# Three small moves in a two-layer decoder trunk: GpSimd's weight sums tied to a norm's last scaling, one pair of transposes put earlier in the embedding, and the MLP's squares written by ScalarE

## The chip, the cores and the metric

The kernel runs on one core of one Trainium2 chip. The metric is the device time of the whole program in microseconds (us), on that core. A core has a matrix engine (TensorE, PE in the profile), three engines that work on vectors (VectorE, DVE; ScalarE, ACT; GpSimd, POOL), a synchronisation engine that issues transfers here (SP), and DMA queues. The engines run their own instruction lists in order and wait for one another through semaphores. Data lies in the on-chip SBUF (the program's "pages", 128 partitions by 512 words) and in the eight PSUM banks into which the matrix engine writes (the program's "banks").

## What is computed

A decoder trunk of two layers on 512 tokens of width 1024. Every sub-layer stands between two RMS norms. Cut to what matters:

```
for i in range(DEPTH):                       # DEPTH = 2
    g = norm_g[i]
    hn = rmsnorm(x, g[0])
    m = fox_attention(...) if i == 0 else short_conv(...)
    x = x + rmsnorm(m, g[1])
    f = jnp.square(jax.nn.relu(rmsnorm(x, g[2]) @ w_up)) @ w_down
    x = x + rmsnorm(f, g[3])
    gate = jax.nn.sigmoid(rmsnorm(x, g[4]) @ w_ple_gate[i])
    e = (p[i] @ w_ple_proj[i]) * gate
    x = x + rmsnorm(e, g[5])
```

The MLP is 1024 to 4096 and back; the last sub-layer is called the embedding below (`ple` in the kernel). Layer 0's mixer is an attention, layer 1's a short convolution.

## The kernel before, in words

**Products.** All matrix products are in full single precision, each as three passes over pairs of a high and a low part (`mm3`, lines 253 to 259): high by high on L255, two mixed ones on L256 and L257. The pair of parts is made by `split` (L261): ScalarE rounds a page to its high part (L263, `wh`, `hTh`, `A11h` ...), another engine subtracts that from the page (L264, `wl`, `hTl`, `A11l` ...). For most weights and for all activations the other engine is VectorE; for the weight sums of the MLP's second matrix, and for two of those of the convolution, it is GpSimd.

**Weights.** `fetch` issues transfers on SP into 14 buffers, `prepare` splits a weight some pages ahead of its use, and `derive` (L155 to L163) forms sums of weight blocks on GpSimd (`dn_T` for the MLP, `c_S` and `b_S` for the convolution), eight instructions for a group of the MLP. These sums exist since the MLP's second product and part of the convolution multiply 2 by 2 blocks by seven products instead of eight.

**A norm.** `pre_norm` (L310 on) runs for each of the four blocks of 128 tokens: ScalarE takes the sums of squares (L286, `junk`), GpSimd the reciprocal root (L278, L281), VectorE scales the block into two pages (`scaled`, L294, `n_h`; `n0b_h` in the norm ahead of the convolution), the matrix engine transposes them (L303, four transposes a page, into `n_p`), and `split` keeps them as `hTh` and `hTl`. The transposes are put off until 46,000 columns have streamed through the matrix engine (`put_off`, `due`), or until a product that reads them calls `need(t)` (L249).

**The MLP** (`mlp`, from L798). Eight groups of 512 hidden units. A group's up product gives four blocks f = 0 to 3: a relu from PSUM on ScalarE (L816, `r`), its square (L802, `q`, on VectorE), and from `q` the parts that the second product needs: `A11` and `A12` directly, `S1` to `S3` after sums on GpSimd (`s`, L830). `down` has 84 matrix instructions a group in groups 0 to 6, seven products in the order of `STEPS`. In group 0 the up product runs in two halves of 256 tokens (16 squares of 128x256 in the two layers) and ScalarE copies the results out to `acc` (L859); in groups 1 to 6 VectorE adds them (L862). Group 7 is plain: ScalarE writes the high part of the square as a square (`hh`, L892), VectorE writes the square again (`q`, L893 by L802) and subtracts (`hl`, L895); meanwhile GpSimd brings the seven sums together (`combine`, L869).

**The embedding** (`ple`, from L919). Four early blocks of `pp`, six matrix instructions each, need nothing of the norm. Then come the eight blocks of `pg`, 24 instructions each, in the order of `BLOCKS`; each begins with `need(t)`. Token block 0 is the first.

**What sets the order.** A scheduler that simulates the program orders each engine's instructions, but keeps what a data dependence or a dependence added by hand asks for. So a change of an engine or of a wait can move rows elsewhere too.

Of the kernel before, what the change touches and what calls it, by code (L numbers as in the profile page):

```python
# [10 lines left out]
AF = mybir.ActivationFunctionType  # L11
ALU = mybir.AluOpType
# [22 lines left out]
FEW = 4  # L35
BLOCKS = ((0, 0), (1, 0), (0, 1), (1, 1), (2, 1), (3, 1), (2, 0), (3, 0))
EARLY = 4
BY_HAND = 2
LEFT = 10
LATE = 0  # L40
# [27 lines left out]
def trunk(ctx: ExitStack, tc, x, pT, g, wv, wqk, bf, wo, wci, wcq, cw, wco, wup, wdn, wpp, wpg, out):  # L68
    nc = tc.nc
# [9 lines left out]
    def page(name, dtype=F32):  # L79
        return pages.tile([P, S], dtype, tag="pg", name=name)  # L80

    def bank(name):
        return psum.tile([P, S], F32, tag="ps", name=name)
# [10 lines left out]

    loads, order, where, ready, fetched, begun = [], [], {}, {}, [], [0]
    derived, recipes = {}, {}

    def plan(key, src):
        where[key] = len(order)
        order.append((key, len(loads)))  # L100
        loads.append(src)
# [45 lines left out]
    def fetch(upto):  # L147
        while len(fetched) < min(upto, len(loads)):
            n = len(fetched)
            raw = raws.tile([P, S], F32, tag="raw", name=f"raw{n}")  # L150
            fetched.append(raw)
            src = loads[n]
            nc.sync.dma_start(raw[:, : src.shape[-1]], src)

    def derive(key):  # L155
        at, sums = recipes.pop(key)
        fetch(max(at.values()) + 1)
        B = {name: fetched[n][:, :S] for name, n in at.items()}
        for name, a, b, op in sums:
            t = page("_".join(str(u) for u in (*key, *name)))  # L160
            derived[(*key, *name)] = t
            B[name] = t[:, :S]
            nc.gpsimd.tensor_tensor(out=B[name], in0=B[a], in1=B[b], op=op)  # L163

    def prepare(upto):
        while begun[0] < min(upto, len(order)):
            n = begun[0]
            begun[0] += 1
            key, at = order[n]
            for of in (key[:3], key[:2]):  # L170
                if of in recipes:
                    derive(of)
            hi, lo = page(f"wh{n}", F32R), page(f"wl{n}", F32R)
            if isinstance(at, tuple):
                raw, w = derived.pop(key), S
                eng = nc.gpsimd if key[0] == "dn" or key[-1] in ON_POOL else nc.vector
            else:
                fetch(at + 1)
                raw, eng, w = fetched[at], nc.vector, loads[at].shape[-1]
                fetched[at] = None  # L180
            split(hi[:, :w], lo[:, :w], raw[:, :w], eng)
            ready[key] = Pair(hi[:, :w], lo[:, :w])

    def wide(*key, soon=SOON):

        prepare(where[key] + 1 + soon)
        return ready[key]
# [61 lines left out]
    def need(*keys):  # L249
        while any(k in keys for _, k, _ in later):  # L250
            later.pop(0)[2]()

    def mm3(ps, a, b, start, stop):

        nc.tensor.matmul(ps, a.hi, b.hi, start=start, stop=False)  # L255
        nc.tensor.matmul(ps, a.lo, b.hi, start=False, stop=False)  # L256
        nc.tensor.matmul(ps, a.hi, b.lo, start=False, stop=stop)  # L257
        streamed[0] += 3 * ps.shape[-1]
        due()
# [24 lines left out]
    def squares(src, name):  # L284
        ss = stat(name)
        nc.scalar.activation(junk, src, AF.Square, scale=D**-0.5, accum_out=ss)  # L286
        return ss
# [3 lines left out]

    def scaled(t, n, xs, r, gB, name):
        h = page(f"{name}_h{t}_{n}")
        nc.vector.scalar_tensor_tensor(  # L294
            out=h[:, :S], in0=xs[n][:, :S], scalar=r, in1=gB[n][:, :S],
            op0=ALU.mult, op1=ALU.mult,
        )
        return h

    def turned(t, n, h, name):  # L300
# [9 lines left out]
    def pre_norm(t, xs, gB, hT, name, also=lambda t, n, ps: None):  # L310

        r = stats(t, xs, name)
        hs = [scaled(t, n, xs, r, gB, name) for n in range(2)]

        def turn():
            for n in range(2):
                ps = turned(t, n, hs[n], name)
                keep(t, n, ps, hT)
                also(t, n, ps)

        put_off(t, turn)
# [7 lines left out]
    def gained(m, gB, n, name, out=None):  # L329

        mg = page(name) if out is None else out
        nc.vector.tensor_tensor(out=mg[:, :S], in0=m, in1=gB[n][:, :S], op=ALU.mult)
        return mg

    def residual(t, mg, sums, xs, name):

        r = rstd(sums, f"{name}_r{t}")
        for n in range(2):
            nc.vector.scalar_tensor_tensor(  # L339
                out=xs[n][:, :S], in0=mg[n][:, :S], scalar=r, in1=xs[n][:, :S],  # L340
                op0=ALU.mult, op1=ALU.add,
            )
# [8 lines left out]
    def tokens_of(pair, t):  # L351
        return pair.at(lambda h: h[:, t * P : (t + 1) * P])

    def tokens(pair, k, t):
        return pair.at(lambda h: h[:, k, t * P : (t + 1) * P])

    def soon(t, n):

        return FEW if n else SOON
# [19 lines left out]
    def attention(hT, first_x, g0, by_hand):  # L379
# [224 lines left out]
        def rows(t):  # L604
            r = stats(t, first_x[t], name)
            return [scaled(t, n, first_x[t], r, g0, name) for n in range(2)]
# [48 lines left out]
        for c in range(-8, n_sc + LAG):  # L655
            if c == n_sc - BY_HAND:
                by_hand.enter_context(tc.manual_schedule(engines={E.PE}))
# [140 lines left out]
    def mlp(l, hT, xs, then, late):  # L798
        acc = {}

        def square(out, r):
            nc.vector.tensor_tensor(out=out, in0=r, in1=r, op=ALU.mult)  # L802

        def up(gr, done, soon=lambda f: SOON):
            for lo, hi in ((0, 256), (256, 512)) if gr == 0 else ((0, 512),):
# [69 lines left out]
        for gr in range(7):  # L875
            A, s, q = {}, {}, {f: page(f"q{l}_{gr}_{f}") for f in range(4)}

            def done(f, lo, hi, r):
                square(q[f][:, lo:hi], r[:, : hi - lo])
                if lo == 0 and f % 2 == 0:  # L880
                    halves(gr, f, ("A11",), q[f], A)
                if hi == S:
                    quarters(gr, f, q, s, A)

            up(gr, done)
            down(gr, A)
# [3 lines left out]
        def done(f, lo, hi, r):  # L890
            h = Pair(*(page(f"h{s}{l}_{f}", F32R) for s in "hl"))
            nc.scalar.activation(h.hi[:, :S], r[:, :S], AF.Square)  # L892
            sq = page(f"q{l}_{f}")  # L893
            square(sq[:, :S], r[:, :S])
            nc.vector.tensor_tensor(  # L895
                out=h.lo[:, :S], in0=sq[:, :S], in1=h.hi[:, :S].bitcast(F32), op=ALU.subtract
            )
            hs.append(h)
            if f == LATE:
                gB.extend(late())  # L900

        up(7, done, lambda f: SOON + 2 * f)
        for t in range(NB):
# [6 lines left out]
            for n in range(2):  # L910
                a = total[t, n][:, :S]
# [7 lines left out]
    def ple(l, hT, xs, gB, then):  # L919
        def proj(t, n):  # L920
            pe = bank(f"pp{l}_{n}_{t}")
            for k in range(2):
                mm3(
                    pe, tokens_of(wide("p", l, k), t),
                    wide("pp", l, n, k), k == 0, k == 1,
                )
            return pe

        early = [proj(t, n) for t, n in BLOCKS[:EARLY]]
        mgs, sums = {}, {}  # L930
        for t, n in BLOCKS:
            need(t)
            if (t, n) == (2, 0):
                prepare(where["pg", l, 1, KT - 1] + 1 + SOON)
            pe = early.pop(0) if early else None
            if pe is None and l == 1 and (t, n) == BLOCKS[-1]:
                pe = proj(t, n)
            ps = bank(f"pg{l}_{n}_{t}")
            for k in range(KT):
                w = wide("pg", l, n, k, soon=soon(t, n))  # L940
                mm3(ps, tokens(hT, k, t), w, k == 0, k == KT - 1)
            gate = page(f"gate{l}_{n}_{t}")
            nc.scalar.activation(gate[:, :S], ps, AF.Sigmoid)
            pe = pe or proj(t, n)
            e = page(f"e{l}_{n}_{t}")
            nc.vector.tensor_tensor(out=e[:, :S], in0=pe, in1=gate[:, :S], op=ALU.mult)
            sums[t, n] = squares(e[:, :S], f"es{l}_{n}_{t}")
            mgs[t, n] = gained(e[:, :S], gB, n, f"em{l}_{n}_{t}")
            if (t, 1 - n) in mgs:
                residual(t, *([d.pop((t, i)) for i in range(2)] for d in (mgs, sums)), xs[t],  # L950
                         f"er{l}")
                then(t)
# [24 lines left out]
    for l in range(2):  # L977
# [46 lines left out]
        else:  # L1024

            def then(t):
                for n in range(2):
                    nc.sync.dma_start(
                        out[t * P : (t + 1) * P, n * S : (n + 1) * S], xs[t][n][:, :S]
                    )  # L1030

        ple(l, h4, xs, g5, then)


# [59 lines left out]
```

## Time and profile before

| | us |
|---|---|
| median of 3 runs | 1248.64 (1248.42 to 1248.65) |
| the profiled execution | 1249.44 |
| its span in the trace | 1247.4 |
| mean granted TensorE clock | 0.996 of full |

The profile is of one execution. A row of the timeline reads: start in us from the span's start, duration in us, engine, line, operation, output and inputs, shapes, and how many; in square brackets the idle time ahead of it and what ended that. Matrix instructions are pipelined: a 128x512 one has a duration of about 0.39 us, yet the next one starts 0.227 us later where nothing is waited for, and that spacing is what counts. A row of the waits reads: who waited, for whom, total us, times, longest. A row of the groups reads: line, engine, operation, names, shapes, count, busy us, mean ns, idle us ahead and what ended it. A row of the chain of waits reads: start, us, engine, line.

### The profile page before, as it was taken

To read this page: it belongs to the slowest core of one execution; us is meant where nothing else is said; L and a number is where in the kernel's file an instruction comes from. 1 tells how busy PE (TensorE), PEld (TensorE's weight loads), DVE (VectorE), ACT (ScalarE), POOL (GpSimd) and SP (SyncE) were. 2 spreads that over 40 slices of the span, in tenths; PEclk is the share of its full clock that TensorE was granted. 3 is DMA by queue.
4 is the path that set the end of the run, shared out by engine and by line. 5 is a ranking of instruction groups with operands and counts; after the bars stand their busy time and mean duration, and the time that the engine had idled before them with its cause. 6 is when DMAs were issued, how large, how long until landed. Compare 5 with 4: busy or idle time off the path is not lost.

```text
span 1247.4 us, 18644 instructions
## 1 busy us (share of the span) xinstructions
PE 1218.7 (98%) x6188; PEld 1030.8 (83%) x6188; DVE 973.7 (78%) x1466; ACT 632.4 (51%) x1357; POOL 692.7 (56%) x667
## 2 busy tenths in 40 slices
PE   7999999999999999999999999999999999999997
PEld 6888887887888888887788999989778888888786
DVE  5657878676789778989878798867788788779972
ACT  5456777546544543454565544544655344535451
POOL 2017667257878776775213255227777878778210
PEclk9999999999999999999999999999999999999999
DMA  7465554532343224428223033542422343236401
GB/s 253 148 159 167 152 156 115 183 121 80 98 135 111 83 77 135 136 68 271 84 85 105 32 102 98 161 164 68 135 68 78 126 136 107 65 100 192 146 18 51
DMA packets 85792, 148.72 MB, mean 119 GB/s; under 512 B 10112, under 2 KB 17328, under 8 KB 85696
## 3 DMA queue, kind: packets, MB, share of 16 engines
q1 hardware_dynamic: 85488, 147.27, 37.5%
q8 instruction: 49, 0.80, 0.3%
q14 instruction: 47, 0.39, 0.1%
q10 hardware_dynamic: 144, 0.26, 0.1%
q0 software_dynamic: 64, 0.00, 0.0%
HBM read 136.93 MB, written 6.37 MB: 115 GB/s over the span
## 4 chain that ended last, share of the span: by engine, by line
PE 71%; DVE 11%; ACT 5%; issue 5%; POOL 4%; DMA 3%; SPq 1%; DVEq 0%; POOLq 0%; ACTq 0%
PE up L255 7%; PE up L257 7%; PE up L256 7%; PE dn L256 6%; PE dn L257 6%; PE dn L255 6%; DVE wl L264 4%; ACT junk L286 2%; PE qk L255 2%; PE qk L256 2%; PE qk L257 2%; PE pg L255 2%; PE pg L256 2%; PE pg L257 2%; DVE n_h L294 1%
## 5 line engine op out<-in xcount | busy, mean ns | idle before, releaser
L264 DVE TENSOR_TENSOR wl<-raw,wh 128x512 fp32r<-128x512 f32 (+1 forms) x398 | 379.2, 1000 | 26.9 <-ACT wh L263 25.8
L263 ACT CAST wh<-raw 128x512 fp32r<-128x512 f32 (+1 forms) x398 | 217.1, 619 | 10.9 <-DVE xd L339 5.0
L256 PE MATMUL up<-hTh,wl 128*128 128x512 f32 (+1 forms) x576 | 210.1, 365 | 0.0
L257 PE MATMUL up<-hTl,wh 128*128 128x512 f32 (+1 forms) x576 | 209.8, 366 | 0.0
L255 PE MATMUL up<-hTh,wh 128*128 128x512 f32 (+1 forms) x576 | 209.3, 366 | 0.0
L264 POOL TENSOR_TENSOR wl<-dn_T,wh 128x512 fp32r<-128x512 f32 x112 | 160.9, 1470 | 35.8 <-ACT wh L263 29.5
L256 PEld LDWEIGHTS up<-hTh,wl 128*128 128x128 f32 x576 | 108.6, 189 | 17.5
L257 PEld LDWEIGHTS up<-hTl,wh 128*128 128x128 f32 x576 | 108.3, 189 | 17.8 <-DVE hTl L264 0.2
L255 PEld LDWEIGHTS up<-hTh,wh 128*128 128x128 f32 x576 | 108.6, 189 | 17.4
L862 DVE TENSOR_TENSOR acc<-dn,acc 128x512 f32<-128x512 f32 x168 | 107.4, 679 | 7.7 <-PE dn L257 7.7
L163 POOL TENSOR_TENSOR dn_T<-raw,raw 128x512 f32<-128x512 f32 x56 | 87.9, 1581 | 39.3 <-DMA raw<-in_wdn 26.4
L816 ACT ACTIVATE r<-up 128x512 f32<-128x512 f32 (+1 forms) x72 | 38.7, 547 | 119.6 <-PE up L257 119.6
L163 POOL TENSOR_TENSOR dn_T<-raw,dn_T 128x512 f32<-128x512 f32 x56 | 91.8, 1638 | 2.2
L802 DVE TENSOR_TENSOR q<-r 128x512 f32<-128x512 f32 (+1 forms) x72 | 70.4, 985 | 27.1 <-ACT r L816 26.7
L263 ACT CAST A11h<-q 128x256 fp32r<-128x256 f32 x28 | 11.4, 407 | 103.2 <-DVE q L802 103.2
L263 ACT CAST wh<-dn_T 128x512 fp32r<-128x512 f32 x112 | 61.2, 617 | 0.0
L255 PE MATMUL pg<-wh,hTh 128*128 128x512 f32 x128 | 51.5, 402 | 3.6 <-ACT hTh L263 3.6
L869 POOL TENSOR_TENSOR acc<-acc,acc 128x512 f32<-128x512 f32 x28 | 47.1, 1716 | 8.7 <-DVE acc L862 8.7
L255 PE MATMUL qk<-hTh,wh 128*128 128x512 f32 x128 | 51.1, 399 | 0.0
L256 PE MATMUL pg<-wh,hTl 128*128 128x512 f32 x128 | 50.9, 398 | 0.0
L257 PE MATMUL qk<-hTl,wh 128*128 128x512 f32 x128 | 50.8, 397 | 0.0
L257 PE MATMUL pg<-wl,hTh 128*128 128x512 f32 x128 | 50.8, 397 | 0.0
(372 smaller groups left out, 3237.0 us busy)
## 6 DMA issues: line engine op xcount, KB each, us to landing
raw<-in_wup SPq DMA_DIRECT2D x128, 256.0 KB, 2.8
raw<-in_wdn SPq DMA_DIRECT2D x128, 256.0 KB, 2.8
raw<-in_wcq SPq DMA_DIRECT2D x36, 256.0 KB, 3.0
raw<-in_wqk SPq DMA_DIRECT2D x32, 256.0 KB, 3.4
raw<-in_wpg SPq DMA_DIRECT2D x32, 256.0 KB, 3.5
g<-in_g SPq DMA_DIRECT2D x22, 256.0 KB, 5.6
prl<-neg_c SPq DMA_DIRECT2D x16, 256.0 KB, 6.5
raw<-in_wo SPq DMA_DIRECT2D x16, 256.0 KB, 4.3
```

Source lines behind the costliest of these rows:

```text
L163: nc.gpsimd.tensor_tensor(out=B[name], in0=B[a], in1=B[b], op=op)
L255: nc.tensor.matmul(ps, a.hi, b.hi, start=start, stop=False)
L256: nc.tensor.matmul(ps, a.lo, b.hi, start=False, stop=False)
L257: nc.tensor.matmul(ps, a.hi, b.lo, start=False, stop=stop)
L263: nc.scalar.copy(hi, src)
L264: eng.tensor_tensor(out=lo, in0=src, in1=hi.bitcast(F32), op=ALU.subtract)
L286: nc.scalar.activation(junk, src, AF.Square, scale=D**-0.5, accum_out=ss)
L294: nc.vector.scalar_tensor_tensor(out=h[:, :S], in0=xs[n][:, :S], scalar=r, in1=gB[n][:, :S], op0=ALU.mult, op1=ALU.mult,)
L802: nc.vector.tensor_tensor(out=out, in0=r, in1=r, op=ALU.mult)
L816: nc.scalar.activation(r[:, :n], ps[:, :n], AF.Relu)
L862: nc.vector.tensor_tensor(out=a, in0=banks[s], in1=a, op=ALU.add)
L869: nc.gpsimd.tensor_tensor(out=a, in0=a, in1=acc[i, s][:, :S], op=ALU.add)
```

## The change

Three edits. First, `scaled` remembers its VectorE instruction in `last_norm`, and the first GpSimd sum that `derive` issues after it gets a dependence on that instruction. In the program's order this concerns the sums of MLP group 0 in both layers (after the second `n_h` of the last token block) and one of the convolution's `c_S` sums (after the last `n0b_h`). GpSimd's list itself keeps its order.

Second, in the embedding `need(BLOCKS[0][0])`, which issues the transposes of token block 0, stands ahead of the third early `pp` block.

Third, `square` is an activation on ScalarE: 72 instructions leave VectorE's list, 56 of 128x512 and 16 of 128x256, and join ScalarE's.

```
+TURNED = 2
...
+    last_norm = []
...
-            nc.gpsimd.tensor_tensor(out=B[name], in0=B[a], in1=B[b], op=op)
+            ins = nc.gpsimd.tensor_tensor(out=B[name], in0=B[a], in1=B[b], op=op)
+            if last_norm:
+                tc.add_manual_dep(
+                    ins.ins, last_norm.pop().ins.name,
+                    mybir.DependencyInfo(mybir.DependencyClass.Sync, mybir.DependencyReason.DATA),
+                )
...
     def scaled(t, n, xs, r, gB, name):
         h = page(f"{name}_h{t}_{n}")
-        nc.vector.scalar_tensor_tensor(
+        last_norm[:] = [nc.vector.scalar_tensor_tensor(
             out=h[:, :S], in0=xs[n][:, :S], scalar=r, in1=gB[n][:, :S],
             op0=ALU.mult, op1=ALU.mult,
-        )
+        )]
         return h
...
         def square(out, r):
-            nc.vector.tensor_tensor(out=out, in0=r, in1=r, op=ALU.mult)
+            nc.scalar.activation(out, r, AF.Square)
...
-        early = [proj(t, n) for t, n in BLOCKS[:EARLY]]
+        early = []
+        for i, (t, n) in enumerate(BLOCKS[:EARLY]):
+            if i == TURNED:
+                need(BLOCKS[0][0])
+            early.append(proj(t, n))
```

The matrix engine's list at the start of layer 0's embedding, before: the end of the third early block `pp_1_0`, the transposes of token block 0 (two rows of four), the fourth early block, and the first product that needs the transposed tokens.

```order
L257 MATMUL pp_1_0_7232<-wl_6935,wh_6865 128x512
L303 MATMUL n_p_0_7239<-ident,n_h_0_7050 128x128 x4
L303 MATMUL n_p_1_7246<-ident,n_h_1_7052 128x128 x4
L255 MATMUL pp_1_1_7253<-wh_6922,wh_6853 128x512
L256 MATMUL pp_1_1_7253<-wh_6922,wl_6854 128x512
L257 MATMUL pp_1_1_7253<-wl_6923,wh_6853 128x512
L255 MATMUL pp_1_1_7253<-wh_6934,wh_6865 128x512
L256 MATMUL pp_1_1_7253<-wh_6934,wl_6866 128x512
L257 MATMUL pp_1_1_7253<-wl_6935,wh_6865 128x512
L255 MATMUL pg_0_0_7260<-wh_6956,hTh 128x512
```

The same place now (nine lines lower in the file): the end of the second early block, the transposes, and the third early block, after which the six rows of the fourth and `pg` follow.

```order
L266 MATMUL pp_0_1_7225<-wl_6890,wh_6865 128x512
L312 MATMUL n_p_0_7232<-ident,n_h_0_7050 128x128 x4
L312 MATMUL n_p_1_7239<-ident,n_h_1_7052 128x128 x4
L264 MATMUL pp_1_0_7246<-wh_6922,wh_6853 128x512
L265 MATMUL pp_1_0_7246<-wh_6922,wl_6854 128x512
L266 MATMUL pp_1_0_7246<-wl_6923,wh_6853 128x512
L264 MATMUL pp_1_0_7246<-wh_6934,wh_6865 128x512
L265 MATMUL pp_1_0_7246<-wh_6934,wl_6866 128x512
L266 MATMUL pp_1_0_7246<-wl_6935,wh_6865 128x512
```

The transposes moved up by six matrix instructions: 12 stand between them and the first `pg` instead of six.

ScalarE's list at the same place, before: sums of squares of the MLP's result (`fs`) and of the new residual (`n_q`, from `xd`), and the casts of the two transposed pages.

```order
L286 ACTIVATE junk,fs_2_0_7134<-acc_4_0_4128 128x512
L286 ACTIVATE junk,fs_2_1_7136<-acc_5_0_4158 128x512
L286 ACTIVATE junk,n_q_2_7146<-xd_2_0_6779 128x512
L263 CAST hTh<-n_p_0_7239 128x4x128
L286 ACTIVATE junk,n_q_2_7148<-xd_2_1_6781 128x512
L263 CAST hTh<-n_p_1_7246 128x4x128
```

And now:

```order
L295 ACTIVATE junk,fs_2_0_7134<-acc_4_0_4128 128x512
L295 ACTIVATE junk,fs_2_1_7136<-acc_5_0_4158 128x512
L272 CAST hTh<-n_p_0_7232 128x4x128
L272 CAST hTh<-n_p_1_7239 128x4x128
L295 ACTIVATE junk,n_q_2_7146<-xd_2_0_6779 128x512
L272 CAST hTh<-n_p_0_7315 128x4x128
```

Both casts moved ahead of the sums of squares of token block 2's residual.

ScalarE's list in MLP group 2 of layer 0, before: relu `r`, and the casts from the square `q`, which VectorE writes.

```order
L263 CAST A11h0_2_0_4740<-q0_2_0_4660 128x256
L816 ACTIVATE r0_2_1_0_4771<-up0_2_1_0_4746 128x512
L263 CAST A12h0_2_1_4774<-q0_2_1_4661 128x512
L263 CAST S1h0_2_1_4782<-s120_2_1_4778 128x512
L263 CAST S3h0_2_1_4786<-s340_2_0_4744 128x512
```

And now:

```order
L811 ACTIVATE q0_2_0_4660<-r0_2_0_0_4737 128x512
L272 CAST A11h0_2_0_4740<-q0_2_0_4660 128x256
L825 ACTIVATE r0_2_1_0_4771<-up0_2_1_0_4746 128x512
L811 ACTIVATE q0_2_1_4661<-r0_2_1_0_4771 128x512
L272 CAST A12h0_2_1_4774<-q0_2_1_4661 128x512
```

The square stands between the relu that it reads and the cast that reads it, on the same engine.

## The prediction

> **What bounds the kernel now.** The page first: which engine is busy nearly always?
>
> ```profile
> span 1247.4 us, 18644 instructions
> PE 1218.7 (98%) x6188; PEld 1030.8 (83%) x6188; DVE 973.7 (78%) x1466; ACT 632.4 (51%) x1357; POOL 692.7 (56%) x667
> ```
>
> The matrix engine is the bound, and no edit takes one of its instructions away. So the change can win only where that engine stands still, runs late or runs slow. The second view is therefore the list of its waits, cut to the places that the edits reach:
>
> ```profile
> PE pg L255 <- ACT hTh L263: 3.6, 2, 1.9
> PE n_p L303 <- DVE n_h L294: 2.3, 4, 1.1
> PE dn L256 <- DVE hl L895: 2.1, 2, 1.2
> PE c L256 <- DVE wl L264: 1.5, 1, 1.5
> PE dn L256 <- DVE A12l L264: 0.6, 2, 0.3
> ```
>
> Together 10.1 us. The other waits of the list lie in the start and in the attention, which no edit touches. A wait list misses small delays and a slow clock, so the third view is the timeline at each of these places, read by the starts of consecutive instructions. For that one needs the spacing where nothing is waited for. A stretch of MLP groups 0 and 1 gives it (columns: window, length, then busy time and count of each engine, granted clock, DMA share):
>
> ```profile
> 306.00:350.00 44.00, 43.73 (x192) 35.56 (x191) 36.29 (x40) 28.88 (x56) 31.95 (x25) 1.00 0.34 104
> ```
>
> 192 matrix instructions in 44.00 us, less one short wait of 0.3, are 0.227 us each.
>
> **Edit 2, the embedding's start.** The matrix engine around the first `pg` of each layer:
>
> ```profile
> 607.64 0.40 PE L257 MATMUL pp<-wl,wh 128*128 128x512 f32 x1
> 609.74 0.50 PE L255 MATMUL pg<-wh,hTh 128*128 128x512 f32 x1 [1.71 <-ACT hTh L263]
> ...
> 1183.43 0.40 PE L257 MATMUL pp<-wl,wh 128*128 128x512 f32 x1
> 1185.76 0.50 PE L255 MATMUL pg<-wh,hTh 128*128 128x512 f32 x1 [1.93 <-ACT hTh L263]
> ```
>
> From start to start 2.10 and 2.33 us instead of 0.227: 1.87 and 2.10 lost, 4.0 together. Why is `hTh` late? ScalarE and VectorE in layer 0:
>
> ```profile
> 608.50 0.63 ACT L286 ACTIVATE junk<-xd 128x512 f32<-128x512 f32 x1 [2.95 <-DVE xd L339]
> ...
> 609.12 0.57 ACT L263 CAST hTh<-n_p 128x512 fp32r<-128x512 f32 x1
> ```
>
> ```profile
> 607.66 1.40 DVE L339 SCALAR_TENSOR_TENSOR xd<-acc,mr_r_y,xd 128x512 f32<-128x512 f32 x2
> ```
>
> ScalarE stood idle for 2.95 us, not for the transposes but for `xd`, the residual of another token block, whose sum of squares is queued ahead of the cast. The order shows that both casts now stand ahead of that sum, and that 12 products instead of six lie between the transposes and `pg`. Six more products are 6 x 0.227 = 1.4 us of cover, and the 2.95 us of ScalarE's idling lie ahead of the casts: together they exceed the 1.71 and 1.93 us waited. Both waits go: **4.0 us**. What is moved late is only that sum of squares; it feeds the norm of block 2, whose transposes come several blocks of `pg` (24 x 0.227 = 5.4 us each) later. Bounds: nothing, if the transposes themselves come to wait for `n_h`, and 4.0.
>
> **The clock behind it.** In layer 1 the wait is followed by slow products. Two adjoining windows:
>
> ```profile
> 1183.56:1186.98 3.42, 1.49 (x9) 1.08 (x8) 2.08 (x4) 2.47 (x7) 0.47 (x2) 1.00 0.01 2
> 1186.98:1190.39 3.41, 3.41 (x10) 2.64 (x9) 3.41 (x6) 1.54 (x5) 1.87 (x3) 0.50 0.00 0
> ```
>
> In the second the granted clock is 0.50 for 3.41 us, so half of it, 1.7 us, is lost. In the window ahead of it the matrix engine was busy for 1.49 of 3.42 us. I read this as the price of the wait in layer 1: without it that window is full, and the clock stays. **1.7 us**; bounds 0 and 1.7. The Trainium skill (TensorE: Matmul & The Clock Gate, "HAM oscillation") has the rule that the clock falls only after idle gaps of over about 3.4 us. This trace does not agree: the gap was 1.93 us. By that rule the slow stretch would have another cause and stay, and the sum would be smaller by its 1.7 us; that is the third rival.
>
> **Edit 1, GpSimd's sums wait.** The chain of waits holds the scalings ahead of both MLPs; the one of 256.29 is the same two instructions for an earlier token block:
>
> ```profile
> 256.29 1.42 DVE n_h L294 x2
> ...
> 270.67 3.46 DVE n_h L294 x2
> ...
> 671.87 1.77 DVE n0b_h L294
> ...
> 847.14 3.46 DVE n_h L294 x2
> ```
>
> ```profile
> 270.60 2.97 POOL L163 TENSOR_TENSOR dn_T<-raw,raw 128x512 f32<-128x512 f32 x2
> ```
>
> The slow pairs (3.46 against 1.42) ran beside GpSimd's first sums, which began 0.07 us earlier. With the wait the scaling takes 1.42, 2.0 us less, and the matrix engine's 2.3 us for `n_p` go. But the sums start at about 272.1 instead of 270.60. Eight of them end later by that 1.5 us less what their own undisturbed speed gives back, and behind them on GpSimd are the low parts of the first weights of `down`. So part of the gain may be handed on to group 0's `down`. That already loses time:
>
> ```profile
> 289.12 0.40 PE L255 MATMUL dn<-wh,A11h 128*128 128x512 f32 x1
> ...
> 310.49 0.39 PE L255 MATMUL up<-hTh,wh 128*128 128x512 f32 x1
> ...
> 865.61 0.40 PE L255 MATMUL dn<-wh,A11h 128*128 128x512 f32 x1
> ...
> 886.98 0.39 PE L255 MATMUL up<-hTh,wh 128*128 128x512 f32 x1
> ```
>
> 84 instructions take 21.37 us in either layer; 84 x 0.227 are 19.07, so 2.3 are lost in each, 4.6 in both. Its waits are for parts made from late squares, which leads to the third edit.
>
> **Edit 3, squares on ScalarE.** In group 0:
>
> ```profile
> 284.35 2.17 ACT L263 CAST wh<-dn_T 128x512 fp32r<-128x512 f32 x4
> ...
> 288.21 0.93 ACT L816 ACTIVATE r<-up 128x256 f32<-128x256 f32 x3
> 291.44 0.62 ACT L263 CAST A12h<-q 128x512 fp32r<-128x512 f32 x1 [2.30 <-DVE q L802]
> ```
>
> ```profile
> 289.23 2.18 DVE L802 TENSOR_TENSOR q<-r 128x256 f32<-128x256 f32 x3
> ```
>
> ScalarE finished three relus at 289.14 and idled 2.30 us for squares that VectorE made one after another beside GpSimd. Done on ScalarE at a relu's price (0.93 / 3 = 0.31) the three relus and squares end at 288.21 + 6 x 0.31 = 290.1, so `A12h` comes 1.4 us earlier. For norm and group 0 together 2.3 + 4.6 = 6.9 us are at stake. I take the norm's 2.3 in full and about half of the 4.6, since the later sums hold back the casts of their results (284.35), which ScalarE has queued ahead of group 0's last relus: **4.5 us**; bounds 0 and 6.9.
>
> In groups 1 to 6 a square costs ScalarE what the existing one (`hh`) costs, and it leaves VectorE, where it cost more:
>
> ```profile
> L802 DVE TENSOR_TENSOR q<-r 128x512 f32<-128x512 f32 x56 | 58.6, 1047 | 23.3 <-ACT r L816 23.0 <-issue 0.2
> ...
> L892 ACT ACTIVATE hh<-r 128x512 fp32r<-128x512 f32 x8 | 5.1, 632 | 0.4
> ```
>
> ```profile
> ACT A11h L263 <- DVE q L802: 103.2, 28, 7.0
> ...
> ACT A12h L263 <- DVE q L802: 41.8, 28, 2.3
> ```
>
> The chain relu, square, cast becomes 0.4 us shorter, and ScalarE's 145.0 us of idling for squares hold the 56 x 0.632 = 35.4 us of new work. In these groups the matrix engine waited only for `A12l`, 0.6 us in group 1 of both layers, with a VectorE list that now lacks a square of 1.05 us: **0.6 us**; bounds 0 and 0.6.
>
> In group 7:
>
> ```profile
> 582.22 0.39 PE L257 MATMUL dn<-wl,hh 128*128 128x512 f32 x1
> 583.86 0.50 PE L256 MATMUL dn<-wh,hl 128*128 128x512 f32 x1 [1.25 <-DVE hl L895]
> ...
> 1158.76 0.39 PE L257 MATMUL dn<-wl,hh 128*128 128x512 f32 x1
> 1159.96 0.50 PE L256 MATMUL dn<-wh,hl 128*128 128x512 f32 x1 [0.81 <-DVE hl L895]
> ```
>
> 1.64 and 1.20 instead of 0.227: 1.41 and 0.97, together **2.4 us**. Ahead of that `hl` VectorE loses three squares at 1.05, over 3 us of queue, while ScalarE adds one of 0.63 to each block: I take it in full. Bounds 0 and 2.4.
>
> The convolution waits 1.5 us for a weight's low part on VectorE, which was queued behind the slowed `n0b_h` (1.77; half of 1.42, 0.71, elsewhere) at the start of its own sums. With the sums held back two scalings are 2.1 us shorter; later sums still run beside later subtractions. I take **1.3 us**; bounds 0 and 1.5.
>
> **The sum.** 4.0 + 1.7 + 4.5 + 0.6 + 2.4 + 1.3 = 14.5 us. The profiled execution took 1249.44 (2.0 around the span of 1247.4), so 1234.9; the median of the runs is 0.8 below it: **1234.1 us**. What a measurement of this kernel can tell from no change is about 0.2%, 2.5 us.
>
> **The rivals.**
>
> *Stalls move.* The matrix engine comes earlier to group 0 and to the convolution, where the weights' low parts come no earlier, since GpSimd started later. Then 4.5 and 1.3 are given back: 8.7 us stay, 1239.9. For it: the sums begin 1.5 us later. Against: they then run without VectorE beside them. Chance 0.17.
>
> *The wait is passed on with its full length.* As before, and each of the two groups 0 starts its `down` 1.5 us later still: 8.7 - 3.0 = 5.7 us, 1242.9. Against: ScalarE casts the first results of the sums only at 284.35, so the sums' late start must first use up that slack. Chance 0.06.
>
> *The slow clock stays*, because a wait elsewhere or the window's place causes it: 14.5 - 1.7 = 12.8, 1235.8. For it: 1.71 us of waiting in layer 0 had no such stretch behind it, so the wait alone does not make one. Chance 0.08.
>
> *All is given back*: ScalarE's longer list delays relus, weight casts or `hTh` at many places by a little. About 1248. Chance 0.04.
>
> *Slower: ScalarE's list becomes the path in groups 1 to 6.* It takes its list in order, so a square behind a relu delays the next weight cast by 0.63. Were the matrix engine to wait for those, four squares in each of 12 groups would cost 12 x 4 x 0.632 = 30 us: about 1264. It decides from 14.5 / 12 = 1.2 us lost in each group. Against it: ScalarE was busy for 28.88 of 44.00 us in the window above, and a group of 180 products (40.9 us) adds 2.5 to its 27. Chance 0.04.
>
> **How the numbers follow.** The forecast has 0.61. The range reaches below to all of the 6.9 and 1.5 us, 2.6 more than taken, and a little of work no longer slowed elsewhere: 1230.5. Above it reaches just over the first rival: 1240.5. This holds the forecast's case, the slow clock's and most of the first rival's: about 0.8. Faster by over 0.2%: 0.61 + 0.17 + 0.08 + 0.06 = 0.92; within: 0.04; slower: 0.04.
>
> **What the changed profile would show.** Right: no wait of `pg` for `hTh`, no half clock at 1187; both `n_h` pairs at 1.4 us; no wait for `hl`; `down` of group 0 under 20.5 us; ScalarE near 54% and VectorE near 73% busy. The group 0 step is wrong if `down` stays over 21 us or if the matrix engine waits for `wl` made from `dn_T`. The whole is wrong if it waits in groups 2 to 6, where it has not waited: for `r`, `A11h` or a `wh`.

## The result, and the profile after

The changed kernel takes 1237.30 us, the median of 5 runs (1236.94 to 1237.49); the kernel before, 1248.64 in the runs beside them (5 runs, 1246.40 to 1251.19). The ratio is 0.9908, with a 95% interval from 0.9897 to 0.9918: 11.3 us faster, inside the range of the prediction, and 3.2 us above its number. The page after:

```profile
span 1235.8 us, 18684 instructions
PE 1213.4 (98%) x6188; PEld 1030.6 (83%) x6188; DVE 896.5 (73%) x1394; ACT 676.1 (55%) x1429; POOL 686.8 (56%) x667
```

VectorE lost 77 us of work and ScalarE gained 44, about as costed, and the span lost 11.6. The matrix engine's waits now (the rows left out lie in the start and in the attention):

```profile
...
PE dn L264 <- ACT r L825: 1.1, 2, 0.9
...
PE n_p L312 <- DVE n_h L303: 0.8, 1, 0.8
PE dn L265 <- DVE S1l L273: 0.8, 2, 0.4
PE c L264 <- DVE za L761: 0.7, 1, 0.7
...
PE dn L265 <- DVE A12l L273: 0.4, 1, 0.4
PE up L266 <- DVE hTl L273: 0.3, 1, 0.3
```

The rows of `pg` for `hTh` and of `dn` for `hl` are gone. The one `n_p` wait left is that of the kernel's start. The waits for the relu `r`, in group 0 of both layers, have risen from 0.5 to 1.1 us, and those for `S1l` and `za` are new. The two starts of the embedding after, `pg` right behind the last `pp` in both layers:

```profile
604.74 0.39 PE L266 MATMUL pp<-wl,wh 128*128 128x512 f32 x1
604.96 0.40 PE L264 MATMUL pg<-wh,hTh 128*128 128x512 f32 x1
...
1175.37 0.39 PE L266 MATMUL pp<-wl,wh 128*128 128x512 f32 x1
1175.59 0.40 PE L264 MATMUL pg<-wh,hTh 128*128 128x512 f32 x1
```

The scaling ahead of layer 0's MLP, from the chain of waits, at 1.43 us for two instructions where it was 3.46:

```profile
257.11 1.41 DVE n_h L303 x2
...
271.47 1.43 DVE n_h L303 x2
```

To see where the time came from, cut the matrix engine's timeline at the starts of its products. The table gives us, from each kernel's profiled execution. "Norm" runs from the MLP's first up product to the first `down`, "group 1" covers groups 1 and 2, "embedding" runs from the first `pp` to the last `pg`, and "convolution" from there to layer 1's MLP. In the headings the wait is edit 1, the turn edit 2 and the squares edit 3:

| section | before | after | turn alone | squares alone | wait alone | no wait | no turn | no squares |
|---|---|---|---|---|---|---|---|---|
| start to layer 0's MLP | 262.40 | 262.89 | 262.25 | 262.21 | 263.06 | 263.93 | 263.59 | 261.59 |
| layer 0: norm, group 0's up | 26.72 | 25.36 | 26.89 | 26.34 | 25.01 | 26.91 | 25.55 | 24.77 |
| group 0's down | 21.36 | 20.95 | 21.35 | 19.07 | 22.57 | 19.07 | 20.95 | 22.49 |
| group 1 | 80.21 | 80.41 | 80.18 | 80.33 | 80.17 | 80.29 | 80.46 | 80.23 |
| group 7's down | 23.61 | 21.76 | 22.95 | 21.76 | 22.41 | 21.76 | 21.76 | 22.18 |
| embedding | 60.41 | 58.40 | 59.71 | 58.37 | 60.35 | 58.40 | 58.37 | 59.63 |
| convolution | 178.53 | 177.50 | 180.18 | 178.28 | 177.33 | 179.03 | 177.21 | 177.49 |
| layer 1: norm, group 0's up | 25.15 | 24.77 | 25.16 | 25.83 | 24.77 | 25.83 | 24.76 | 24.77 |
| group 0's down | 21.37 | 20.33 | 21.40 | 19.07 | 21.96 | 19.07 | 20.30 | 21.95 |
| group 1 | 80.25 | 80.68 | 80.22 | 80.28 | 80.21 | 80.35 | 80.71 | 80.19 |
| group 7's down | 22.86 | 21.76 | 22.33 | 21.76 | 22.16 | 21.76 | 21.76 | 22.44 |
| embedding | 61.77 | 57.93 | 59.17 | 57.95 | 60.28 | 57.97 | 57.94 | 59.31 |

The columns on the right are the first experiments. Groups 3 to 6 and group 7's up are left out; they are equal to 0.01 us in all kernels. What follows the last `pg` takes 8.3 to 8.8 us. The first row holds no edit and still spreads by 2.3 us, most of it in the attention. That is why total times of kernels 1 us apart can't be told apart, while most sections can.

From before to after, the embeddings gain 2.0 and 3.8 us (the slow clock in the second), group 7 gains 1.85 and 1.1, norm with group 0 1.8 and 1.4, and the convolution 1.0. Group 1 costs 0.2 and 0.4, and start and end 0.8. The sum is 11.6.

### The profile page after: what moved, and what is told of

Its sections match the earlier page's. It is cut to its first block, busy times and chain, and to the rows that moved or that the text cites. A ratio compares the mean times of both kernels' runs of the same rounds, so it can differ in the third digit from the quotient of the medians.

```text
span 1235.8 us, 18684 instructions
## 1 busy us (share of the span) xinstructions
PE 1213.4 (98%) x6188; PEld 1030.6 (83%) x6188; DVE 896.5 (73%) x1394; ACT 676.1 (55%) x1429; POOL 686.8 (56%) x667
## 4 chain that ended last, share of the span: by engine, by line
PE 89%; DVE 3%; POOL 2%; ACT 2%; issue 2%; DMA 2%; SPq 0%; POOLq 0%; DVEq 0%; ACTq 0%
PE up L266 9%; PE up L265 9%; PE up L264 9%; PE dn L265 8%; PE dn L266 8%; PE dn L264 8%; PE pg L265 2%; PE pg L264 2%; PE pg L266 2%; PE qk L264 2%; PE qk L265 2%; PE qk L266 2%; PE co L264 1%; PE co L266 1%; PE co L265 1%
## 5 line engine op out<-in xcount | busy, mean ns | idle before, releaser
L273 DVE TENSOR_TENSOR wl<-raw,wh 128x512 fp32r<-128x512 f32 (+1 forms) x398 | 370.2, 975 | 27.5 <-ACT wh L272 26.3
L273 POOL TENSOR_TENSOR wl<-dn_T,wh 128x512 fp32r<-128x512 f32 x112 | 155.0, 1417 | 32.6 <-ACT wh L272 32.6
L273 DVE TENSOR_TENSOR A12l<-q,A12h 128x512 fp32r<-128x512 f32 x28 | 23.3, 833 | 51.7 <-ACT A12h L272 51.7
L273 DVE TENSOR_TENSOR A11l<-q,A11h 128x256 fp32r<-128x256 f32 x28 | 25.9, 926 | 45.5 <-ACT A11h L272 45.5
L265 PE MATMUL qk<-hTh,wl 128*128 128x512 f32 x128 | 50.2, 393 | 0.0
```

The source lines that it names most:

```text
L273: eng.tensor_tensor(out=lo, in0=src, in1=hi.bitcast(F32), op=ALU.subtract)
```

## The experiments

### Each edit alone, and the wait left out

**The turn alone.** Both other edits are undone (the first removed line stands for the several of edit 1).

```
-            ins = nc.gpsimd.tensor_tensor(...); if last_norm: tc.add_manual_dep(...)
+            nc.gpsimd.tensor_tensor(out=B[name], in0=B[a], in1=B[b], op=op)
...
-            nc.scalar.activation(out, r, AF.Square)
+            nc.vector.tensor_tensor(out=out, in0=r, in1=r, op=ALU.mult)
```

> Edit 2 alone (transposes of the embedding's first block put earlier; squares on VectorE, GpSimd's sums without the wait). My theory: both waits of the first pg for hTh go (4.0 us) and with them the half clock that follows in layer 1 (1.7 us), independently of the other two edits: 5.7 to 5.9 us below the kernel before, about 1242.8 us, and no stretch at 0.50 in the embedding. Rival (the slow clock has another cause): 4.0 us, about 1244.6 us, with a half-clock stretch of 3.4 us still near the start of layer 1's embedding.

Measured 1245.30, 0.9978 of the kernel before (0.9968 to 0.9989): 2.7 us, half of what I expected, and neither theory's number. The clock stayed up in the embedding, so the rival as stated falls. But a new wait stands a few instructions behind the removed one, in layer 0:

```profile
609.07 0.50 PE L260 MATMUL pg<-wh,hTl 128*128 128x512 f32 x1 [1.02 <-DVE hTl L268]
```

```profile
607.01 1.40 DVE L343 SCALAR_TENSOR_TENSOR xd<-acc,mr_r_y,xd 128x512 f32<-128x512 f32 x2
608.34 1.27 DVE L268 TENSOR_TENSOR hTl<-n_p,hTh 128x512 fp32r<-128x512 f32 x2
```

`hTh` was cast early, but its low part is VectorE's, and there it is queued behind the same residual `xd` that ScalarE had been waiting for.

And the slow clock is not gone from this profile. It stands in layer 1's convolution, behind waits of 1.29 and 0.48 us that the edit does not touch:

```profile
672.30:675.71 3.41, 1.64 (x12) 1.26 (x11) 3.41 (x3) 2.98 (x6) 2.57 (x2) 1.00 0.26 71
675.71:679.12 3.41, 3.41 (x18) 3.41 (x18) 3.41 (x7) 0.51 (x1) 0.00 (x0) 0.50 0.71 212
```

That is half of 3.41, 1.7 us, and the convolution of this kernel is 1.65 us longer than before. Whether other executions have it there is not known.

**The squares alone.** The wait and the turn are undone, so only edit 3 is left.

> Edit 3 alone (squares on ScalarE; no wait of the sums, transposes of the embedding where they were). My theory: group 7's waits for hl go (2.9 us by starts), group 1 loses 0.2 to 0.4 us more in each layer as in the changed kernel, and group 0 gains about 1 us in all while the wait for n_h stays: 3 to 4 us below the kernel before, about 1245 us. Rival (the squares need the wait of edit 1 to bring anything in group 0, or cost as much elsewhere as they bring in group 7): under 1.5 us, about 1247.5 us.

Measured 1236.61, 0.9909 (0.9893 to 0.9925): 11.4 us, all that the three edits bring together. My theory was off by 8 us, on the side that neither theory held. The embedding's two starts wait for no `hTh` and no `hTl`. ScalarE there in layer 0:

```profile
601.67 1.07 ACT L267 CAST hTh<-n_p 128x512 fp32r<-128x512 f32 x2 [2.03 <-PE n_p L307]
602.63 0.65 ACT L290 ACTIVATE junk<-xd 128x512 f32<-128x512 f32 x1
```

The matrix engine's list has the transposes where they were before, six products ahead of `pg`. But ScalarE's list has both casts ahead of the sum of squares. VectorE still makes `hTl` right behind `xd`, as in the turn alone, but `xd` itself comes earlier:

```profile
592.66 1.42 DVE L298 SCALAR_TENSOR_TENSOR n_h<-xd,n_r_y,g 128x512 f32<-128x512 f32 x2 [0.27 <-POOL n_r_y L285]
...
601.75 1.40 DVE L343 SCALAR_TENSOR_TENSOR xd<-acc,mr_r_y,xd 128x512 f32<-128x512 f32 x2
603.08 1.27 DVE L268 TENSOR_TENSOR hTl<-n_p,hTh 128x512 fp32r<-128x512 f32 x2
```

The embedding's first `pp` starts at 596.94 here, so this `xd` starts 4.8 us behind it; in the kernel before and in the turn alone it is 6.1 and 6.2. The first scaling of the norm shows the other order of the list: here it stands 4.3 us ahead of the first `pp`, in the kernel before 1.1 us, behind other work of VectorE:

```profile
598.43 1.45 DVE L332 TENSOR_TENSOR acc<-acc,g 128x512 f32<-128x512 f32 x2 [0.78 <-ACT junk L286]
599.79 0.68 DVE L912 TENSOR_TENSOR acc<-dn,acc 128x512 f32<-128x512 f32 x1
600.39 1.40 DVE L294 SCALAR_TENSOR_TENSOR n_h<-xd,n_r_y,g 128x512 f32<-128x512 f32 x2
```

So with the squares elsewhere the scheduler put the lists of both engines in another order. No run moves the squares and keeps the old order, or the reverse, so how much of the gain is the order's is not shown. Group 0's `down` is at its full speed, 19.07 us, in both layers.

**The wait alone.** The turn and the squares are undone.

> Edit 1 alone (GpSimd's first sum waits for the norm's last scaling; squares on VectorE). My theory: the scalings fall from 3.46 to 1.42 us a pair and the convolution's start gains 1.0 us, but with VectorE making the squares late in group 0 the norm's gain is mostly handed on to group 0's down: 1 to 2 us below the kernel before, about 1247 us. Rival (the wait by itself costs group 0 more than the norm gains): the kernel before or slower, 1248.6 to 1250 us, with down of group 0 at 23 us or more instead of 21.4. Second rival (nothing is handed on): 3.5 us below, about 1245 us.

Measured 1244.85, 0.9970 (0.9958 to 0.9982): 3.1 us, more than the theory's 1 to 2 and near the second rival's 3.5. But the sections show that time is handed on, so the second rival's number is met for another reason. The convolution gains 1.2 and the norms 1.7 and 0.4; 1.2 and 0.6 go back in group 0's `down`, 22.57 and 21.96 us, as the theory said (less than the rival's 23). The rest lies where this edit changes nothing: 1.2 and 0.7 in group 7, and 1.5 in layer 1's embedding, where this profile has no slow stretch.

**No wait.** The changed kernel without edit 1.

> The changed kernel without edit 1. My theory: the scalings take 3.46 us a pair again, the convolution gives back 1.0 us and norm with group 0 about 1 to 2 us of their 3.2: 1239.3 to 1240.3 us. Rival (the stall only moves from the norm to down, so the wait in the MLP is worth nothing): 1237.5 to 1238.3 us.

Measured 1238.21, 0.9914 (0.9900 to 0.9927), which can't be told from the changed kernel's 0.9908. The sections can be told apart: without the wait the norm sections are 1.55 and 1.06 longer and group 0's `down` 1.88 and 1.26 shorter. In the MLP the wait costs 0.3 and 0.2 us; the rival holds there. In the convolution it brings 1.5 here, and 1.1 where the turn is left out too (178.28 with the squares alone, 177.21 with wait and squares).

### The turn and the squares left out

**No turn.**

> The changed kernel without edit 2 (wait and squares alone). My theory now: once the squares are off VectorE the embedding's first hTh is ready in time whatever stands in the matrix engine's list, so edit 2 is worth nothing beside edit 3: 1237.3 us, within 1 us, no wait of pg for hTh. Rival (edit 2 is needed when the sums wait, as the prediction had it): 4 to 5.7 us more, 1241 to 1243 us.

Measured 1237.76, 0.9918 (0.9905 to 0.9930), with the embeddings at 58.37 and 57.94, as with the turn: it is worth nothing beside the squares.

**No squares.**

> The changed kernel without edit 3 (wait and turn alone). My theory: the gains of the two alone add up, 2.7 and 3.1 us, less what overlaps in nothing: about 1242.5 us; group 0's down at 22 to 22.6 us and the embedding's first pg waiting about 1 us for hTl. Rival (edit 2 needs edit 3 to bring its 5.7 us, or the two disturb each other): 1244.5 us or more.

Measured 1243.69, 0.9968 (0.9956 to 0.9979): 3.3 us below the kernel before in the same runs, between the two numbers. The sections are those of the two edits alone: 59.63 and 59.31 in the embedding with the wait for `hTl`, 22.49 and 21.95 in group 0. So in these sections they do not disturb each other. The medians of the two alone add up to 5.8 us and not to 3.3; the three intervals leave room for that.

### Where the changed kernel still waits

In layer 0's group 0 `down` loses 1.9 us against its 19.07, and 0.85 of it in one wait. The matrix engine, ScalarE and GpSimd there:

```profile
293.52 0.39 PE L266 MATMUL dn<-wl,A12h 128*128 128x512 f32 x1
294.76 0.50 PE L264 MATMUL dn<-wh,S1h 128*128 128x512 f32 x1 [0.85 <-ACT r L825]
```

```profile
292.99 0.62 ACT L272 CAST S1h<-s 128x512 fp32r<-128x512 f32 x1 [2.21 <-POOL s L839]
293.81 0.62 ACT L272 CAST S3h<-s 128x512 fp32r<-128x512 f32 x1 [0.20 <-POOL s L839]
294.34 0.38 ACT L825 ACTIVATE r<-up 128x256 f32<-128x256 f32 x1
```

```profile
273.02 2.55 POOL L167 TENSOR_TENSOR dn_T<-raw,raw 128x512 f32<-128x512 f32 x2 [1.58 <-DVE n_h L303]
...
285.05 5.25 POOL L273 TENSOR_TENSOR wl<-dn_T,wh 128x512 fp32r<-128x512 f32 x4
290.25 0.74 POOL L839 TENSOR_TENSOR s<-q 128x256 f32<-128x256 f32 x1
```

Read backwards: the relu that the product waits for stands behind `S1h` in ScalarE's list, `S1h` waits 2.21 us for the quarter sums `s`, and GpSimd reaches these only after eight weight sums and four low parts. The first of the weight sums waited 1.58 us for `n_h`. So edit 1's delay is handed on over two engines.

**Quarter sums on VectorE.** Group 0 alone:

```
-            sums = lambda out, a, b, op: nc.gpsimd.tensor_tensor(out=out, in0=a, in1=b, op=op)
+            eng = nc.vector if gr == 0 else nc.gpsimd
+            sums = lambda out, a, b, op: eng.tensor_tensor(out=out, in0=a, in1=b, op=op)
```

> The changed kernel, with the quarter sums s of MLP group 0 on VectorE instead of GpSimd. My theory: with the wait of edit 1, group 0's down is late because GpSimd reaches the quarter sums only after the late weight sums and four low parts, and ScalarE's last relus are queued behind the casts of those quarter sums; VectorE idles there. The down falls from 20.95 and 20.33 us to 19.1 to 19.6: 2 to 2.5 us less, about 1235 us. Rival (the weight casts or the banks hold it, or VectorE's sums are slowed by GpSimd's): 1237 us or more, down at 20.5 us.

Measured 1234.26, 0.9894 (0.9881 to 0.9907). Group 0's `down` takes 19.92 and 19.25 instead of 20.95 and 20.33; in layer 0 that is 0.3 above the expected range. VectorE, idle there, makes the first sum in 1.14 us and the next three in 0.42 each:

```profile
288.29 1.14 DVE L840 TENSOR_TENSOR s<-q 128x256 f32<-128x256 f32 x1 [0.30 <-ACT q L811]
...
290.27 0.42 DVE L840 TENSOR_TENSOR s<-q,q 128x256 f32<-128x256 f32 x1
290.72 0.42 DVE L840 TENSOR_TENSOR s<-s,q 128x256 f32<-128x256 f32 x1
291.18 0.42 DVE L840 TENSOR_TENSOR s<-q,s 128x256 f32<-128x256 f32 x1
```

**The same without the wait**, which tells whether these sums help by themselves:

> The changed kernel without edit 1, with group 0's quarter sums on VectorE. My theory: these sums matter only because edit 1 makes GpSimd late; without it group 0's down already takes 19.07 us, so they bring nothing: the same as without edit 1, about 1238 us, with the waits for n_h (3.0 us) still there. Rival (VectorE's quarter sums help by themselves): 1236 us or less.

Measured 1238.32, 0.9919 (0.9904 to 0.9933), and `down` at 19.07 in both layers: they bring nothing, as expected. The quarter sums hold `down` up only because of edit 1.

**Group 1's low parts.** VectorE of the changed kernel there:

```profile
336.82 1.29 DVE L871 TENSOR_TENSOR acc<-dn,acc 128x512 f32<-128x512 f32 x2 [5.24 <-PE dn L266]
338.03 0.83 DVE L273 TENSOR_TENSOR A12l<-q,A12h 128x512 fp32r<-128x512 f32 x1
339.68 0.69 DVE L871 TENSOR_TENSOR acc<-dn,acc 128x512 f32<-128x512 f32 x1 [0.82 <-PE dn L266]
340.29 1.53 DVE L273 TENSOR_TENSOR S1l<-s,S1h 128x512 fp32r<-128x512 f32 x1
```

It idles for 5.24 us ahead of two accumulations that need the matrix engine's first product, and the low parts, which need only ScalarE, stand behind them in its list. `S1l` then takes 1.53 us beside GpSimd's `wl`. The edit keeps them in front (`add` is the accumulation, `lows` holds the low parts):

```
...
+                        first = {1: "A12", 2: "S1"}.get(i)
+                        if gr == 1 and first:
+                            tc.add_manual_dep(
+                                add.ins, lows[gr, first].ins.name,
+                                mybir.DependencyInfo(mybir.DependencyClass.Sync, mybir.DependencyReason.DATA),
+                            )
```

> The changed kernel, with a dependence in MLP group 1 that keeps VectorE's first accumulations behind the low part A12l, and the second pair behind S1l. My theory: the waits for A12l and S1l in group 1 (0.25 + 0.56 us in layer 0, 0.53 + 0.55 in layer 1) are only a matter of VectorE's order, since it idled for 5.2 us with the inputs ready: they go, 1.5 to 1.9 us less, about 1235.5 us. Rival (the accumulations that are now later hold the banks, or S1l is slow beside GpSimd wherever it stands): no gain or a loss, 1237 to 1238 us.

Measured 1234.55, 0.9899 (0.9883 to 0.9915): group 1's sections are 79.33 in both layers instead of 80.41 and 80.68, 2.4 us in all, more than the 1.9 of the four waits expected to go. VectorE now:

```profile
331.93 0.91 DVE L273 TENSOR_TENSOR A12l<-q,A12h 128x512 fp32r<-128x512 f32 x1 [1.50 <-ACT A12h L272]
335.65 1.29 DVE L871 TENSOR_TENSOR acc<-dn,acc 128x512 f32<-128x512 f32 x2 [2.81 <-PE dn L266]
336.86 1.31 DVE L273 TENSOR_TENSOR S1l<-s,S1h 128x512 fp32r<-128x512 f32 x1
```

**Both together.**

> The changed kernel with both additions: group 0's quarter sums on VectorE, and group 1's first accumulations kept behind A12l and S1l. My theory: the two places are apart and each stall is ended where it stands, so the gains add, by sections 1.0 + 1.1 in group 0, 1.1 + 1.35 in group 1, and 0.5 around them: 1231.5 to 1233 us. Rival (the matrix engine, earlier at group 1, finds weights or banks not ready): 1234 us, no better than either alone.

Measured 1231.89, 0.9869 (0.9851 to 0.9887): the fastest kernel of this study by its median, 5.4 us under the changed one. Group 0's `down` takes 19.87 and 19.26, group 1 79.33 twice: by sections the gains add.

**The wait in the convolution only**, with the squares and without the turn:

```
-            if last_norm:
+            if key[0] != "dn" and last_norm:
```

> Edit 3, and of edit 1 only the part in the convolution (the sums of MLP group 0 do not wait; transposes where they were). My theory: the MLP's wait is worth -0.2 to -0.3 us a layer and the convolution's wait 0.8 to 1.5 us, so this is the best cut of the three edits as they stand: 1235.3 to 1236.3 us, convolution section 177.3 to 177.5, norm with group 0's down 45.4 to 46.0 and 44.9. Rival (the convolution's gain is within its spread from run to run): 1236.6 us or more.

Measured 1236.69, 0.9906 (0.9890 to 0.9923): 0.4 us above the expected range, and not to be told from the squares alone. The convolution's section is 177.23 and layer 0's norm with group 0 45.44, both as expected, but layer 0's group 1 took 80.97, 0.6 more than with the squares alone, with a wait of 0.64 for `A12l`. VectorE's list there is in the same order in both kernels, and `A12l` ran beside GpSimd's `wl` in both, but took 1.38 us here and 0.73 there. Why is not shown.

### The slow clock once more

> The kernel before, profiled once more, for the half-clock stretch in layer 1's embedding. My theory: the wait there is 1.9 us again, and the stretch of 3.4 us at 0.50 follows it again. Rival (it depends on where the wait falls in a window of the clock's own, since waits of 1.62 to 1.71 us elsewhere had none): a wait of 1.9 us without a slow stretch. Time 1246 to 1251 us.

The profiled execution took 1248.32. It has the wait of 1.90 us at the same place in layer 1, and the slow stretch behind it again. Two windows there:

```profile
1182.20:1185.60 3.40, 1.50 (x8) 0.95 (x8) 2.09 (x4) 2.29 (x7) 0.30 (x1) 1.00 0.01 2
1185.60:1189.03 3.43, 3.43 (x10) 2.64 (x9) 3.40 (x6) 1.72 (x5) 2.04 (x3) 0.50 0.00 0
```

Layer 0's wait in the same execution had none, and neither had the kernel with the wait alone, where layer 1's `pg` waits a little less:

```profile
609.24 0.50 PE L255 MATMUL pg<-wh,hTh 128*128 128x512 f32 x1 [1.76 <-ACT hTh L263]
```

```profile
1182.60 0.50 PE L264 MATMUL pg<-wh,hTh 128*128 128x512 f32 x1 [1.62 <-ACT hTh L272]
```

```profile
1180.40:1183.90 3.50, 1.88 (x11) 1.27 (x10) 2.43 (x5) 2.55 (x7) 0.55 (x2) 1.00 0.01 2
1183.90:1187.30 3.40, 3.40 (x18) 2.83 (x17) 3.40 (x6) 2.05 (x6) 1.79 (x3) 1.00 0.00 0
```

So two waits of 1.90 and 1.93 us were followed by it, and those of 1.62 to 1.76 us in the embedding were not. But the length alone does not decide: in the turn alone it followed waits of 1.29 and 0.48 us, and without the wait (the run "no wait") 1.75 us at the same place in the convolution had none:

```profile
668.50:671.91 3.41, 1.66 (x15) 1.42 (x14) 3.41 (x3) 3.23 (x7) 3.41 (x3) 1.00 0.01 2
```

In the three profiles with the stretch in layer 1 the matrix engine was busy for 1.49, 1.50 and 1.64 of the 3.4 us just ahead; here, with 1.66, it stayed away. These few would fit a decision by how busy a window of 3.4 us is, and then where the window falls counts too. It is no rule yet: at the end of the program, in the second profile of the kernel before, a window with 1.47 us had no slow stretch right behind it.

## Why the prediction was right or wrong

- **The bound: right.** The matrix engine's work is unchanged, and 11.6 us of its lost time went, nearly all at places named, if not always by the edit named. Groups 2 to 6 lost nothing: ScalarE's list did not become the path.
- **Embedding and clock: the size right, the cause wrong.** Foretold 4.0 + 1.7, measured 5.85 by sections. But I gave it to edit 2, and the runs show that edit 3 alone brings it, that edit 2 alone brings 0.7 + 2.6 us there, and nothing beside edit 3. The step that failed is "Both waits go: 4.0 us": I followed `hTh` on ScalarE, whose new order I had read in the kernel with all three edits, and did not follow `hTl` through VectorE's list, nor ask which edit had moved the casts. That the size came out right is luck: the three edits were made together, and another of them did it.
- **The slow clock: the place right, the cause only in part.** The stretch in layer 1's embedding went wherever the wait of 1.9 us there went, and the changed kernel has none there. But the third rival, a wait elsewhere or the window's place, has a point: in the turn alone a stretch of the same length stands in the convolution. The rule of the Trainium skill (TensorE: Matmul & The Clock Gate, "HAM oscillation") that only idle gaps over about 3.4 us matter does not agree with two profiles of the kernel before, where 1.90 and 1.93 us came just ahead of 3.4 us at 0.50. Nor does it agree with the turn alone, where the longest gap ahead was 1.29 us.
- **Group 7: right**, 2.95 for 2.4; the starts of two single instructions missed smaller delays in the section. Its section also moves by 0.5 to 0.7 us between profiles of the kernel before.
- **Norm and group 0: 3.2 for 4.5, the largest miss.** Two errors. The 2.3 us of the `n_p` row held 0.8 us of the kernel's start, which no edit touches: a row of the waits adds up all places with the same names. And "about half of the 4.6" for `down` was a guess between bounds; 1.45 came back, since the wait that speeds the scalings makes GpSimd late. The list of waits had one more row of group 0, `dn` for `r` with 0.5 us, which the prediction put down to the start and the attention; it is the row that doubled. And the sign "`down` under 20.5 us" failed in layer 0, with 20.95. The rival "stalls move" had this mechanism right for the MLP, and only there: in the convolution the wait paid.
- **Group 1: wrong in sign.** Foretold 0.6 gained, measured 0.6 lost. The step that failed is the "VectorE list that now lacks a square": `A12l` did not stand behind a square but behind accumulations that wait for the matrix engine, so an emptier list ends no sooner. Most of the loss comes with wait and squares together: the squares alone lose 0.15, the wait alone nothing.
- **Convolution: 1.0 for 1.3**, the size a little off.
- **Left out: 0.8 us** at start and end, within what the attention spreads.

The sum of 14.5 was thus 2.9 too high in the profiled execution: 1.3 from norm and group 0, 1.2 from group 1, 0.3 from the convolution, 0.8 from start and end, less 0.7 in the embedding and group 7.

## What to carry to other kernels

When several edits meet at one wait, cost each as if the others were absent: a wait ends when the last of its inputs comes, and here one edit already brought all that another was for. An instruction held back on one in-order engine is paid for wherever that engine's next results are needed, so follow the queue behind it to the end, over the second engine too. And before counting on an emptier list, look at what the late instruction is queued behind: work removed from a list doesn't help one that stands behind a wait.

## What the runs showed of the hardware

- VectorE can be slowed by GpSimd: its scalings took 3.46 us a pair beside GpSimd's sums and 1.43 without, and a low part of 128x512 1.53 us beside GpSimd against 0.69 alone. Not every instruction is: with the squares alone `A12l` took 0.73 us beside GpSimd's `wl`.
- A sum of 128x256 took VectorE 0.42 us in most cases and up to 1.14, where GpSimd took 0.73 to 1.20.
- The clock was halved for 3.4 us after waits of only 1.90 and 1.93 us, twice at the same place, and once after 1.29 and 0.48 us; 1.75 us had no such stretch behind it.
